# Latent attention's scores: one product over 128 rows a head in place of two over 64 and 32 rows

## The chip, the cores and the metric

The kernel runs on one core of a Trainium2 chip. The metric is the device time of one execution in microseconds. Several executions are timed, and one more is taken with the hardware profiler, which gives the rows shown below. TensorE (PE) multiplies, VectorE (DVE) and ScalarE (ACT) do the elementwise work and empty the accumulators (PSUM banks), SyncE (SP) issues the loads, and GpSimd (POOL) issues the gathers at the end.

## What is computed

Two blocks run one after the other on 256 tokens of 1024 features, in float32. The first block has two layers; each holds a gated recurrence of eight heads (HGRN), a causal latent attention of eight heads (MLA), and a cross-attention to a memory. The second block (a dilated attention, a pooling mixer and a routed feed-forward that gathers 256 rows of 2048 floats for each of 128 partitions) isn't touched by the change. The part that matters:

```python
q = (_rmsnorm(cq, q_norm) @ w_uq).reshape(B, S, 8, 64 + 32)
q_nope, q_rope = q[..., :64], _rope(q[..., 64:], cos, sin)
c = _rmsnorm(ckv, kv_norm)
k_nope = (c @ w_uk).reshape(B, S, 8, 64)
v = (c @ w_uv).reshape(B, S, 8, 64)
k_rope = _rope(kr, cos, sin)              # one key of 32 for all heads
s = (einsum(q_nope, k_nope) + einsum(q_rope, k_rope)) / sqrt(96)
p = softmax(where(causal, s, -1e30)); o = einsum(p, v)
# _rope: [t1*cos - t2*sin, t1*sin + t2*cos] over the two halves of 16
```

## The kernel before, in words

Weights stream through three buffers as half units of 128x1024 floats. Each is loaded on SP's queue (`raw`, L167), rounded by ScalarE into `wh` (L159), and the remainder is taken by VectorE into `wl` (L160); a product is then three passes on TensorE (`mm3`, L213 to L215). After each half unit `tick` emits side work: Python generators that stand in a list and yield an estimated cost, against a credit per tick. `mla_qkv`, `mla_rest`, `mla_attend`, the HGRN levels (L328 to L390) and the gates are such side work. `behind` (`bh` in the code) ties a VectorE instruction in order, without a semaphore, behind the newest split `wl` that was emitted. The framework then orders each engine's instructions by a simulation of its own, and each engine works through its list strictly in order.

In a layer, `layer` loads `ws`, the small weights of the latent attention (L636), forms the latent rows (`misc`), and starts the side work. `mla_rest` transposes the latents (L499), projects q in three banks (L512) that ScalarE empties into `qn` and `qr` (L514, L516), k in two banks into `kn` (L522, L523), v in two (L527, L528), rotates `qr` by a product with a permutation (L532) and three VectorE steps (L536, L537, L539), and rotates the shared key into `kr`, repeated four times down the partitions (L543 to L553). `lnr`, the rows of the layer norm, has the buffer of `ws`, so its load (L641) waits on SP's queue for the last product that reads `ws`.

`mla_attend` calls `attend` eight times, for two blocks of queries and four pairs of heads (h, h+4). Each call writes the scores of two heads into one bank. A head takes one product over 64 rows (`qn`, `kn`, L563) and one over 32 rows (`qr`, `kr`, L565), which accumulate; there are 128 keys for the first block of queries and 256 for the second. A float32 product is two MATMUL instructions in the trace. Then come the mask, the softmax, the transposes (L437) and the product with v (L461).

Of the kernel before, what the change touches and what calls it, by code (L numbers as in the profile page):

```python
# [8 lines left out]
F = mybir.dt.float32  # L9
# [3 lines left out]
AF = mybir.ActivationFunctionType  # L13
OP = mybir.AluOpType
# [4 lines left out]
S = 256  # L19
D = 1024  # L20
# [77 lines left out]
def pack(inp):  # L98

    g = {k: np.asarray(v) for k, v in inp.items()}  # L100
    o = {}
    o["ca"], o["cb"] = _shape_constants()
    o["x"] = g["x"].reshape(2, 128, D).transpose(1, 0, 2)
    o["memT"] = g["mem"][0].T.reshape(8, 128, S).transpose(1, 0, 2)
    o["pos"] = g["positions"].reshape(1, S)
    wu, wm, ws = [], [], []
    for l in range(NL):
        w = g["w_in"][l]
        m = w[:, OCQ:OMG].reshape(2, 4, 128, 416).transpose(0, 2, 1, 3).reshape(2, 128, 1664)
        wm.append(m)  # L110
        u = _fm(g["w_mem_k"][l], 0, 512) + _tm(g["w_mem_v"][l], 0, 512)
        pair = lambda j: _fm(w, OF + 256 * j, 256) + _fm(w, OQ + 256 * j, 256)
        u += pair(0) + _tm(w, OI, 512) + pair(1) + _tm(w, OG, 512) + pair(2) + _tm(w, OI + 512, 512) + pair(3)
        u += _fm(w, OMQ, 512) + _tm(w, OG + 512, 512) + _tm(w, OMEMG, 512) + _tm(w, OMG, 512)
        wo = g["w_out"][l].reshape(4, 4, 128, 2, 512)
        for kg in KORD:
            for cg in range(2):
                u.append(wo[kg, :, :, cg].transpose(1, 0, 2).reshape(128, 2048))
        wu.append(np.stack(u))
        uq = g["w_mla_uq"][l].reshape(2, 128, 8, 96)  # L120
        uq = np.concatenate([uq[..., :64].reshape(2, 128, 512), uq[..., 64:].reshape(2, 128, 256)], axis=-1)
        ws.append(np.concatenate([uq.transpose(1, 0, 2).reshape(128, 1536), g["w_mla_uk"][l], g["w_mla_uv"][l]], axis=1))
    o["wu"], o["wm"], o["ws"] = np.stack(wu), np.stack(wm), np.stack(ws)
    o["rows1"] = np.concatenate([g["hgrn_out_norm"], g["mla_q_norm"], g["mla_kv_norm"], g["ln_g"], g["ln_b"]], axis=1)
    o["lnc"] = np.stack([g["ln_g"], g["ln_b"]], axis=1).reshape(2, 2, 8, 128).transpose(3, 0, 1, 2)
    o["lbl"] = g["hgrn_lb_logits"].reshape(2, 8, 128).transpose(2, 0, 1)
    cols = [g["c_2"].reshape(8, 128).T, g["norm1_g_2"].reshape(8, 128).T, g["norm2_g_2"].reshape(8, 128).T,
            g["pool_scale_2"].reshape(4, 128).T, g["b_ada_2"].reshape(48, 128).T]
    o["cols2"] = np.concatenate(cols, axis=1)
    o["rows2"] = np.concatenate([g["b_ada_2"][0, 2048:3072], g["b_ada_2"][0, 5120:6144], g["final_g_2"]]).reshape(1, 3072)  # L130
    o["wada"] = g["w_ada_2"][0].reshape(8, 128, 6, 1024).transpose(2, 0, 1, 3)
    w2 = g["w_in_2"][0]
    u = _fm(w2, 0, 1024) + _tm(w2, 1024, 1024)
    wo = g["w_out_2"][0].reshape(2, 4, 128, 2, 512)
    for kg in (1, 0):
        for cg in range(2):
            u.append(wo[kg, :, :, cg].transpose(1, 0, 2).reshape(128, 2048))
    u += _fm(g["peer_wq_2"][0], 0, 2048)
    o["wu2"] = np.stack(u)
    o["ws2"] = np.concatenate([g["pool_w_2"][0].transpose(1, 0, 2).reshape(128, 512),  # L140
                               g["peer_subkeys_2"][0].transpose(2, 0, 1).reshape(128, 256)], axis=1)
    o["puv"] = np.concatenate([g["peer_u_2"][0], g["peer_v_2"][0]], axis=1)
    return {k: np.ascontiguousarray(v) for k, v in o.items()}


class Prog:
# [346 lines left out]
    def mla_rest(self, ws, cn, out):  # L493
        nc, bh = self.nc, self.behind
        cT = self.ml.tile([128, 3, S], F, name="cT")
        for k in range(3):
            ps = self.pps.tile([128, S], F, name="bank")
# [1 line left out]
                nc.tensor.transpose(ps[:, tt * 128:(tt + 1) * 128], cn[:, tt, k * 128:(k + 1) * 128], self.ident)  # L499
            nc.scalar.activation(cT[:, k, :], ps, AF.Copy)  # L500
            yield 0.3
        sc = 1.0 / math.sqrt(96)
        qn = self.ml.tile([128, 4, S], F, name="qn")
        qr = self.ml.tile([128, 2, S], F, name="qr")
        kn = self.ml.tile([128, 4, S], F, name="kn")
        v = self.ml.tile([128, 2, 512], F, name="v")
        for j in range(3):
            ps = self.pps.tile([128, 2, S], F, name="bank")
            for m in range(2):
                for k in range(2):  # L510
                    c = k * 768 + (2 * j + m) * 128
                    nc.tensor.matmul(ps[:, m, :], ws[:, c:c + 128], cT[:, k, :], start=k == 0, stop=k == 1)  # L512
            if j < 2:
                nc.scalar.activation(qn[:, 2 * j:2 * j + 2, :], ps, AF.Copy, scale=sc)  # L514
            else:
                nc.scalar.activation(qr, ps, AF.Copy, scale=sc)  # L516
            yield 0.6
        for j in range(2):
            ps = self.pps.tile([128, 2, S], F, name="bank")
            for m in range(2):  # L520
                c = 1536 + (2 * j + m) * 128
                nc.tensor.matmul(ps[:, m, :], ws[:, c:c + 128], cT[:, 2, :], start=True, stop=True)  # L522
            nc.scalar.activation(kn[:, 2 * j:2 * j + 2, :], ps, AF.Copy)  # L523
            yield 0.6
        for tt in range(2):
            ps = self.pps.tile([128, 512], F, name="bank")
            nc.tensor.matmul(ps, cT[:, 2, tt * 128:(tt + 1) * 128], ws[:, 2048:2560], start=True, stop=True)  # L527
            nc.scalar.activation(v[:, tt, :], ps, AF.Copy)  # L528
            yield 0.6

        ps = self.pps.tile([128, 2, S], F, name="bank")
        nc.tensor.matmul(ps, self.perm, qr, start=True, stop=True)  # L532
        tmp = self.h2.tile([128, 2, S], F, name="pt")
        sb = self.sin[:, None, :].to_broadcast([128, 2, S])
        cb = self.cos[:, None, :].to_broadcast([128, 2, S])
        bh(nc.vector.tensor_tensor(tmp, ps, sb, op=OP.mult))  # L536
        bh(nc.vector.tensor_tensor(qr, qr, cb, op=OP.mult))  # L537
        yield 1.2
        bh(nc.vector.tensor_tensor(qr, qr, tmp, op=OP.add))  # L539
        yield 0.6  # L540
        ps = self.pps.tile([32, S], F, name="bank")
        for tt in range(2):
            nc.tensor.transpose(ps[:, tt * 128:(tt + 1) * 128], cn[:, tt, 384:416], self.ident)  # L543
# [2 lines left out]
        ps = self.pps.tile([128, 2, S], F, name="bank")  # L546
        nc.tensor.matmul(ps[:, 0, :], self.rep[:32, :], kr0, start=True, stop=True)
        nc.tensor.matmul(ps[:, 1, :], self.reps[:32, :], kr0, start=True, stop=True)
        kr = self.ml.tile([128, S], F, name="kr")
        tk = self.h2.tile([128, S], F, name="pt")  # L550
        bh(nc.vector.tensor_tensor(kr, ps[:, 0, :], self.cos, op=OP.mult))
        bh(nc.vector.tensor_tensor(tk, ps[:, 1, :], self.sin, op=OP.mult))
        bh(nc.vector.tensor_tensor(kr, kr, tk, op=OP.add))  # L553
        out += [qn, qr, kn, kr, v]
        yield 1.0

    def mla_attend(self, qkv, y):
        nc = self.nc
        qn, qr, kn, kr, v = qkv

        def score(ps, h, tt, nk):
            a, c = h // 2, (h % 2) * 64
            nc.tensor.matmul(ps, qn[c:c + 64, a, tt * 128:(tt + 1) * 128], kn[c:c + 64, a, :nk], start=True, stop=False)  # L563
            a, c = h // 4, (h % 4) * 32
            nc.tensor.matmul(ps, qr[c:c + 32, a, tt * 128:(tt + 1) * 128], kr[c:c + 32, :nk], start=False, stop=True)  # L565

        def bias(s, ps, heads, tt):
            n = len(heads)
# [61 lines left out]
    def layer(self, l, x, xt, mem):  # L630
        nc, I = self.nc, self.I
        W = I["wu"][l]
        rows = self.h4.tile([128, 512], F, name="rowsa", bufs=1)
        nc.sync.dma_start(rows, I["rows1"][l:l + 1, 0:512].to_broadcast([128, 512]))
        ws = self.ml.tile([128, 2560], F, name="ws")
        nc.sync.dma_start(ws, I["ws"][l])  # L636
        pm = self.misc(l, xt)
        qkv = []
# [35 lines left out]
        v = values()  # L674
# [3 lines left out]
        g = self.silu_gate(tok())  # L678
# [4 lines left out]
        v = values()  # L683
# [49 lines left out]
        if l == NL - 1:  # L733
            self.drain()
            self.ahead = self.unit(I["wu2"][0][:, 0:1024])
            ss = [self.sm.tile([128, 3], F, name="nss") for _ in range(2)]
        for tt in range(2):
            residual(tt, 0)
# [62 lines left out]
    def setup(self, cp, c0):  # L801
# [39 lines left out]
        self.pin = nc.scalar.preload_act_table_set("natural_log_exp_and_others")  # L841
        self.tc.add_manual_dep(self.pin.ins, last.ins.name, NOSYNC, reason="the set is loaded behind the sines")
        nc.vector.tensor_scalar(self.sin, self.sin, cols[:, 1:2], None, op0=OP.mult)

        lg = cp.tile([128, 2, 8], F, name="lg")
        nc.sync.dma_start(lg, I["lbl"])
# [378 lines left out]
def body(tc, I, O, stop=None):  # L1225
    nc = tc.nc
    p = Prog(tc, I)
    with tc.tile_pool(name="c0", bufs=1) as c0, tc.tile_pool(name="wp", bufs=3) as wp, \
# [4 lines left out]
        with tc.tile_pool(name="mo", bufs=1) as mo:  # L1233
            xnp = tc.alloc_tile_pool(name="xnp", bufs=1)
            gp = tc.alloc_tile_pool(name="gp", bufs=1)
            p.xn = xnp.tile([128, 2, D], F, name="xn")
            with tc.tile_pool(name="cp", bufs=1) as cp, tc.tile_pool(name="xtp", bufs=4) as xtp, tc.tile_pool(name="h4", bufs=3) as h4, \
                    tc.tile_pool(name="h2", bufs=2) as h2, tc.tile_pool(name="ml", bufs=1) as ml:
                p.xtp, p.h4, p.h2, p.ml = xtp, h4, h2, ml
# [47 lines left out]
```

## Time and profile before

| | us |
|---|---|
| median of 3 runs | 1469.14 (1466.65 to 1471.23) |
| profiled execution | 1465.43 |
| its span, first to last instruction | 1463.7 |
| PE busy in the span | 1292.2 (88%) |
| DVE busy | 1014.7 (69%) |
| ACT busy | 591.9 (40%) |

The time of the profiled execution is 1.7 us more than its span. "PE busy" counts matmuls whose ends are modelled, so a busy PE can still be short of its best rate; PEld is the loading of the stationary operand, which can overlap the product before it.

### The profile page before, as it was taken

Reading aid. Unit: us, or ns where it says so; the run is one execution under the profiler, and the core shown is the slowest. Engines: PE = TensorE matmul, PEld = TensorE weight load, DVE = VectorE, ACT = ScalarE, POOL = GpSimd, SP = SyncE. Lnnn points to the kernel's source line nnn. Section 1 sums busy time; section 2 is a strip of 40 time slices with the busy share of each in tenths; the row PEclk is TensorE's granted clock in tenths of the full one; section 3 lists DMA queues with packets and bytes.
Section 4 is the critical chain, followed back from the end, with each engine's and each line's share of the span. In section 5 each row is a group of like instructions: output and inputs, shape, how many; then the busy total and the mean of one; then the engine's idle time right before and its main releaser. Section 6 shows DMA issues by size and latency. Waiting matters only on the chain.

```text
span 1463.7 us, 17364 instructions
## 1 busy us (share of the span) xinstructions
PE 1292.2 (88%) x5834; PEld 882.2 (60%) x5834; DVE 1014.7 (69%) x2039; ACT 591.9 (40%) x1288; POOL 243.5 (17%) x260
## 2 busy tenths in 40 slices
PE   8999999998999999989997997786888777878776
PEld 7888897777887888878677733232333333333332
DVE  6487689767578787576566777777776977755554
ACT  5556556535566576344544422222222322211112
POOL 0000000000000000000003243333334333333330
PEclk9999999999999999999998999999889898999988
DMA  8564255576562453556538799999999999999993
GB/s 290 167 208 129 87 172 163 178 242 220 165 188 87 130 159 101 173 197 214 179 123 343 290 423 421 421 421 421 421 421 421 377 421 421 422 420 422 422 421 158
DMA packets 74537, 404.79 MB, mean 277 GB/s; under 512 B 8912, under 2 KB 9296, under 8 KB 40784
## 3 DMA queue, kind: packets, MB, share of 16 engines
q0 software_dynamic: 36864, 268.45, 44.3%
q1 hardware_dynamic: 37584, 135.23, 28.2%
q8 instruction: 47, 0.77, 0.2%
q14 instruction: 42, 0.34, 0.1%
HBM read 402.60 MB, written 1.05 MB: 276 GB/s over the span
## 4 chain that ended last, share of the span: by engine, by line
PE 49%; DMA 36%; DVE 7%; issue 3%; ACT 3%; POOL 0%; DVEq 0%; POOLq 0%; ACTq 0%
DMA uv<-in_puv_dram,eid 31%; PE bank L214 9%; PE bank L213 9%; PE bank L215 9%; PE acc L1218 7%; DMA raw<-in_wu_dram 4%; PE bank L371 3%; ACT wh L159 2%; PE bank L461 2%; DVE uv L1208 2%; DVE wl L160 1%; PE bank L221 1%; PE bank L565 1%; PE bank L563 1%; PE bank L437 1%
## 5 line engine op out<-in xcount | busy, mean ns | idle before, releaser
L1218 PE MATMUL acc<-uv,d 128*128 128x512 f32 x1024 | 501.7, 649 | 126.1 <-ACT d L1216 125.7
L1218 PEld LDWEIGHTS acc<-uv,d 128*128 128x128 f32 x1024 | 207.6, 208 | 415.3 <-issue 245.5
L1174 POOL DMA_INDIRECT uv<-in_puv_dram,eid x256 | 243.3, 950 | 1183.1 <-DVE eid L1113 774.5
L1208 DVE CUSTOM_DVE_ANT_0 uv<-hid,uv 128x1024 f32<-128x1024 f32 x256 | 313.2, 1223 | 180.7 <-DMA uv<-in_puv_dram,eid 172.2
L160 DVE TENSOR_TENSOR wl<-raw,wh 128x1024 fp32r<-128x1024 f32 (+1 forms) x184 | 223.2, 1214 | 123.9 <-ACT wh L159 115.5
L159 ACT ACTIVATE wh<-raw 128x1024 fp32r<-128x1024 f32 (+1 forms) x184 | 192.8, 1050 | 196.1 <-DMA raw<-in_wu_dram 79.6
L1211 ACT ACTIVATE dot<-dot 128x4 f32<-128x4 f32 (+1 forms) x66 | 13.5, 205 | 408.9 <-DVE dot L1208 408.8
L213 PE MATMUL bank<-wh,xh 128*128 128x512 f32 (+1 forms) x400 | 161.6, 405 | 1.2 <-ACT xh L258 0.8
L214 PE MATMUL bank<-wl,xh 128*128 128x512 f32 (+1 forms) x400 | 160.0, 400 | 2.0 <-DVE wl L160 2.0
L215 PE MATMUL bank<-wh,xl 128*128 128x512 f32 (+1 forms) x400 | 159.1, 398 | 0.0
L213 PE MATMUL bank<-xh,wh 128*128 128x256 f32 x384 | 113.5, 296 | 3.8 <-ACT wh L159 3.8
L215 PE MATMUL bank<-xh,wl 128*128 128x256 f32 x384 | 110.6, 288 | 4.8 <-DVE wl L160 4.8
L214 PE MATMUL bank<-xl,wh 128*128 128x256 f32 x384 | 110.6, 288 | 0.0
L1216 ACT ACTIVATE d<-ident,dot 128x128 f32<-128x128 f32 x256 | 82.8, 390 | 39.9 <-DVE dot L1212 34.0
L214 PEld LDWEIGHTS bank<-wl,xh 128*128 128x128 f32 x400 | 75.6, 189 | 18.5 <-DVE wl L160 3.4
L213 PEld LDWEIGHTS bank<-wh,xh 128*128 128x128 f32 x400 | 75.6, 189 | 16.6 <-ACT xh L258 1.0
L215 PEld LDWEIGHTS bank<-wh,xl 128*128 128x128 f32 x400 | 75.6, 189 | 15.7 <-issue 0.7
L213 PEld LDWEIGHTS bank<-xh,wh 128*128 128x128 f32 x384 | 73.9, 192 | 6.8 <-ACT wh L159 4.8
L215 PEld LDWEIGHTS bank<-xh,wl 128*128 128x128 f32 x384 | 73.7, 192 | 6.4 <-DVE wl L160 6.0
L214 PEld LDWEIGHTS bank<-xl,wh 128*128 128x128 f32 x384 | 73.9, 192 | 1.8 <-issue 1.2
L213 PE MATMUL bank<-nh,wh 128*128 128x256 f32 x192 | 58.5, 305 | 1.1 <-issue 0.7
L214 PE MATMUL bank<-nl,wh 128*128 128x256 f32 x192 | 56.5, 295 | 1.4 <-DVE nl L259 1.4
(286 smaller groups left out, 1715.1 us busy)
## 6 DMA issues: line engine op xcount, KB each, us to landing
raw<-in_wu_dram SPq DMA_DIRECT2D x176, 512.0 KB, 4.2
raw<-in_wada_dram SPq DMA_DIRECT2D x48, 512.0 KB, 3.5
uv<-in_puv_dram,eid POOLq DMA_INDIRECT x256, 18.0
raw<-in_wm_dram SPq DMA_DIRECT2D x8, 416.0 KB, 4.0
ws<-in_ws_dram SPq DMA_DIRECT2D x2, 1280.0 KB, 9.2
raw<-in_memT_dram SPq DMA_DIRECT2D x4, 512.0 KB, 4.6
lnr<-in_rows_dram SPq DMA_DIRECT2D x2, 1024.0 KB, 7.9
cb<-in_cb_dram SPq DMA_DIRECT2D x1, 1408.0 KB, 6.0
```

The source lines that it names most:

```text
L159: nc.scalar.activation(wh[:, :n], raw[:, :n], AF.Copy)
L160: self.last_split = nc.vector.tensor_tensor(wl[:, :n], raw[:, :n], wh[:, :n].bitcast(F), op=OP.subtract)
L213: mm(ps, a[0], b[0], start=start, stop=False)
L214: mm(ps, a[0], b[1], start=False, stop=False)
L215: self.last_mm = mm(ps, a[1], b[0], start=False, stop=stop)
L221: m = self.nc.tensor.matmul(ps, self.zero, self.zero[:, None, :].to_broadcast([128, 4, 128]), start=True, stop=True)
L371: nc.tensor.matmul(ps[:, h, k, :], st[:, c:c + 128], mv[:, c:c + 128], start=True, stop=True)
L461: nc.tensor.matmul(po[:, i, :], pt[:, i * kb + k, :], v[:, k, h * dv:(h + 1) * dv], start=k == 0, stop=k == kb - 1)
L1174: nc.gpsimd.indirect_dma_start(out=t, out_offset=None, in_=I["puv"], in_offset=bass.IndirectOffsetOnAxis(ap=eid[:, u, k:k + 1], axis=0))
L1208: self.last_split = nc.vector.tensor_tensor_reduce(out=uv[:, 0:D], in0=hid, in1=uv[:, 0:D], scale=1.0, scalar=0.0, op0=OP.mult, op1=OP.add ...
L1216: nc.scalar.activation(d, self.ident, AF.Copy, scale=dot[:, u, k:k + 1])
L1218: nc.tensor.matmul(acc[:, cg * 512:(cg + 1) * 512], d, uv[:, D + cg * 512:D + (cg + 1) * 512], start=u % 8 == 0 and k == 0, stop=u % 8 == ...
```

## The change

The weights of q are packed per head as 128 columns: 64 plain ones, the 32 rotary ones, and the rotary ones again with their halves exchanged. So q comes out of four banks as eight tiles of 128 rows, and one VectorE multiplication by a table `turn` (scale; scale times cosine; scale times signed sine) empties each bank. The key tile `kt` has the head's 64 plain rows below and the rotated shared key twice above, copied in for all heads by two ScalarE instructions. The score of a head is then one product over 128 rows. The product with the permutation and the three VectorE steps of the rotation of q go. k is projected head by head into 64 columns; k and v come after the rotation of the key. `ws` grows from 2560 to 3072 floats a partition. `kt` takes the buffer that `xn`, a tile used from the end of the second layer on, held alone; `xn` is allocated when it is needed. The change's short description also names routing steps tied behind dot products; no line of the diff touches the routing.

```diff
@@ pack
-        uq = np.concatenate([uq[..., :64].reshape(2, 128, 512), uq[..., 64:].reshape(2, 128, 256)], axis=-1)
+        uq = np.concatenate([uq, uq[..., 80:], uq[..., 64:80]], axis=-1).reshape(2, 128, 1024)
@@ mla_rest
-        qn = self.ml.tile([128, 4, S], F, name="qn")
-        qr = self.ml.tile([128, 2, S], F, name="qr")
-        kn = self.ml.tile([128, 4, S], F, name="kn")
+        q = self.ml.tile([128, 8, S], F, name="q")
+        kt = self.xnp.tile([128, 8, S], F, name="kt", tag="xn")
-        for j in range(3):
+        for j in range(4):
...
-            if j < 2:
-                nc.scalar.activation(qn[:, 2 * j:2 * j + 2, :], ps, AF.Copy, scale=sc)
-            else:
-                nc.scalar.activation(qr, ps, AF.Copy, scale=sc)
+            bh(nc.vector.tensor_tensor(q[:, 2 * j:2 * j + 2, :], ps, self.turn[:, None, :].to_broadcast([128, 2, S]), op=OP.mult))
...
-        nc.tensor.matmul(ps, self.perm, qr, start=True, stop=True)
-        bh(nc.vector.tensor_tensor(tmp, ps, sb, op=OP.mult))
-        bh(nc.vector.tensor_tensor(qr, qr, cb, op=OP.mult))
-        bh(nc.vector.tensor_tensor(qr, qr, tmp, op=OP.add))
...
+        for j in range(2):
+            nc.scalar.activation(kt[64:, 4 * j:4 * j + 4, :], kr[64:, None, :].to_broadcast([64, 4, S]), AF.Copy)
+        for j in range(4):
+            ps = self.pps.tile([64, 2, S], F, name="bank")
+            for m in range(2):
+                c = 2048 + (2 * j + m) * 64
+                nc.tensor.matmul(ps[:, m, :], ws[:, c:c + 64], cT[:, 2, :], start=True, stop=True)
+            nc.scalar.activation(kt[:64, 2 * j:2 * j + 2, :], ps, AF.Copy)
+            yield 0.3
+        # v as before, now last
@@ mla_attend, score
-            nc.tensor.matmul(ps, qn[c:c + 64, a, tt * 128:(tt + 1) * 128], kn[c:c + 64, a, :nk], start=True, stop=False)
-            nc.tensor.matmul(ps, qr[c:c + 32, a, tt * 128:(tt + 1) * 128], kr[c:c + 32, :nk], start=False, stop=True)
+            nc.tensor.matmul(ps, q[:, h, tt * 128:(tt + 1) * 128], kt[:, h, :nk], start=True, stop=True)
@@ layer
-        ws = self.ml.tile([128, 2560], F, name="ws")
+        ws = self.ml.tile([128, 3072], F, name="ws")
@@ setup
+        self.turn = cp.tile([128, S], F, name="turn")
+        nc.vector.memset(self.turn[:64, :], sc)
+        nc.vector.tensor_scalar(self.turn[64:96, :], self.cos[64:96, :], sc, None, op0=OP.mult)
+        nc.vector.tensor_scalar(self.turn[96:, :], self.sin[96:, :], sc, None, op0=OP.mult)
```

## Rows read from the trace of the kernel before

**Rows 1.** Page, the span in 40 slices: busy tenths of PE.

```profile
PE   8999999998999999989997997786888777878776
```

**Rows 2.** Stages: us, busy (instructions) of PE, PEld, DVE, ACT, POOL; clock; DMA.

```profile
420.00:490.00 70.00, 69.97 (x443) 57.18 (x442) 51.48 (x95) 42.23 (x106) 0.00 (x0) 0.98 0.35 108
...
112.00:138.50 26.50, 26.36 (x186) 23.01 (x184) 20.46 (x39) 18.19 (x45) 0.00 (x0) 1.00 0.42 139
138.50:175.00 36.50, 36.50 (x209) 28.20 (x208) 25.74 (x50) 20.48 (x52) 0.00 (x0) 0.91 0.23 73
```

**Rows 3.** Chain that ended last, 110 to 200 us: start, us, what.

```profile
111.49 0.89 PE bank L371 x8
112.38 0.41 PE bank L563 x2
112.79 0.41 PE bank L565 x2
...
114.04 0.31 PE bank L213
114.35 0.11 PE bank L214
...
138.72 0.63 PE bank L563 x2
...
169.63 0.62 PE bank L565 x2
```

**Rows 4.** Instructions by line and shape, whole span.

```profile
L565 PE MATMUL bank<-kr,qr 32*128 32x256 f32 x32 | 11.3, 434 | 0.0
```

**Rows 5.** Chain, 50 to 110 us: the projections and small products.

```profile
52.71 4.75 PE bank L512 x22
...
63.69 0.86 PE bank L532 x2
...
90.59 0.61 PE bank L374 x8
91.20 0.31 PE bank L213
```

**Rows 6.** Three short stretches of the layers; columns as in rows 2.

```profile
160.50:163.90 3.40, 3.40 (x14) 3.11 (x14) 2.63 (x5) 1.72 (x7) 0.00 (x0) 0.50 0.25 65
170.70:174.10 3.40, 3.40 (x15) 3.17 (x15) 1.38 (x3) 3.12 (x7) 0.00 (x0) 0.51 0.41 134
464.30:467.70 3.40, 3.40 (x13) 2.68 (x12) 2.29 (x5) 0.57 (x2) 0.00 (x0) 0.50 0.15 60
```

**Rows 7.** DVE and ACT in order of time; idle before in brackets.

```profile
60.16 1.23 DVE L160 TENSOR_TENSOR wl<-raw,wh 128x1024 fp32r<-128x1024 f32 x1 [8.24 <-ACT wh L159]
64.58 0.69 DVE L536 TENSOR_TENSOR pt<-bank,sin 128x512 f32<-128x512 f32 x1 [1.79 <-PE bank L532]
...
58.36 0.60 ACT L523 ACTIVATE kn<-bank 128x512 f32<-128x512 f32 x1 [0.27 <-PE bank L522]
59.07 1.06 ACT L159 ACTIVATE wh<-raw 128x1024 fp32r<-128x1024 f32 x1
```

**Rows 8.** SP's queue, the two loads of `lnr`, and what the first waited for.

```profile
63.72 0.33 SPq L641 DMA_DIRECT2D lnr<-in_rows_dram  x1
377.21 0.33 SPq L641 DMA_DIRECT2D lnr<-in_rows_dram  x1
SPq L641 <- PE bank L527: 0.6, 1, 0.6
```

**Rows 9.** The load of `ws`: size and landing; its second issue, its first use.

```profile
ws<-in_ws_dram SPq DMA_DIRECT2D x2, 1280.0 KB, 9.2
352.07 0.33 SPq L636 DMA_DIRECT2D ws<-in_ws_dram  x1
364.41 5.78 PE L512 MATMUL bank<-cT,ws 128*128 128x256 f32 x24
```

**Rows 10.** The instructions that write the rotated key last: ns, first and last start.

```profile
L553 DVE TENSOR_TENSOR kr<-kr,pt x2: 398/400/402, 77.0 to 390.5; 128x256 f32<-128x256 f32 x2
```

More of the change, by code (lines that the diff above doesn't have):

```diff
@@ L120, in pack @@
         uq = g["w_mla_uq"][l].reshape(2, 128, 8, 96)
-        uq = np.concatenate([uq[..., :64].reshape(2, 128, 512), uq[..., 64:].reshape(2, 128, 256)], axis=-1)
-        ws.append(np.concatenate([uq.transpose(1, 0, 2).reshape(128, 1536), g["w_mla_uk"][l], g["w_mla_uv"][l]], axis=1))
+        uq = np.concatenate([uq, uq[..., 80:], uq[..., 64:80]], axis=-1).reshape(2, 128, 1024)
+        ws.append(np.concatenate([uq.transpose(1, 0, 2).reshape(128, 2048), g["w_mla_uk"][l], g["w_mla_uv"][l]], axis=1))
     o["wu"], o["wm"], o["ws"] = np.stack(wu), np.stack(wm), np.stack(ws)
@@ L501, in mla_rest @@
             yield 0.3
-        sc = 1.0 / math.sqrt(96)
-        qn = self.ml.tile([128, 4, S], F, name="qn")
-        qr = self.ml.tile([128, 2, S], F, name="qr")
-        kn = self.ml.tile([128, 4, S], F, name="kn")
+        q = self.ml.tile([128, 8, S], F, name="q")
+        kt = self.xnp.tile([128, 8, S], F, name="kt", tag="xn")
         v = self.ml.tile([128, 2, 512], F, name="v")
-        for j in range(3):
+        for j in range(4):
             ps = self.pps.tile([128, 2, S], F, name="bank")
@@ L510, in mla_rest @@
                 for k in range(2):
-                    c = k * 768 + (2 * j + m) * 128
+                    c = k * 1024 + (2 * j + m) * 128
                     nc.tensor.matmul(ps[:, m, :], ws[:, c:c + 128], cT[:, k, :], start=k == 0, stop=k == 1)
-            if j < 2:
-                nc.scalar.activation(qn[:, 2 * j:2 * j + 2, :], ps, AF.Copy, scale=sc)
-            else:
-                nc.scalar.activation(qr, ps, AF.Copy, scale=sc)
+            bh(nc.vector.tensor_tensor(q[:, 2 * j:2 * j + 2, :], ps, self.turn[:, None, :].to_broadcast([128, 2, S]), op=OP.mult))
             yield 0.6
[L518 to L531, printed above, removed]
-        nc.tensor.matmul(ps, self.perm, qr, start=True, stop=True)
-        tmp = self.h2.tile([128, 2, S], F, name="pt")
-        sb = self.sin[:, None, :].to_broadcast([128, 2, S])
-        cb = self.cos[:, None, :].to_broadcast([128, 2, S])
-        bh(nc.vector.tensor_tensor(tmp, ps, sb, op=OP.mult))
-        bh(nc.vector.tensor_tensor(qr, qr, cb, op=OP.mult))
-        yield 1.2
-        bh(nc.vector.tensor_tensor(qr, qr, tmp, op=OP.add))
-        yield 0.6
         ps = self.pps.tile([32, S], F, name="bank")
@@ L548, in mla_rest @@
         nc.tensor.matmul(ps[:, 1, :], self.reps[:32, :], kr0, start=True, stop=True)
-        kr = self.ml.tile([128, S], F, name="kr")
         tk = self.h2.tile([128, S], F, name="pt")
+        bh(nc.vector.tensor_tensor(tk, ps[:, 1, :], self.sin, op=OP.mult))
+        kr = self.h2.tile([128, S], F, name="pt")
         bh(nc.vector.tensor_tensor(kr, ps[:, 0, :], self.cos, op=OP.mult))
-        bh(nc.vector.tensor_tensor(tk, ps[:, 1, :], self.sin, op=OP.mult))
         bh(nc.vector.tensor_tensor(kr, kr, tk, op=OP.add))
-        out += [qn, qr, kn, kr, v]
         yield 1.0
+        for j in range(2):
[7 more added lines that the diff above has]
+            yield 0.3
+        for tt in range(2):
+            ps = self.pps.tile([128, 512], F, name="bank")
+            nc.tensor.matmul(ps, cT[:, 2, tt * 128:(tt + 1) * 128], ws[:, 2560:3072], start=True, stop=True)
+            nc.scalar.activation(v[:, tt, :], ps, AF.Copy)
+            yield 0.6
+        out += [q, kt, v]
     def mla_attend(self, qkv, y):
         nc = self.nc
-        qn, qr, kn, kr, v = qkv
+        q, kt, v = qkv
         def score(ps, h, tt, nk):
-            a, c = h // 2, (h % 2) * 64
-            nc.tensor.matmul(ps, qn[c:c + 64, a, tt * 128:(tt + 1) * 128], kn[c:c + 64, a, :nk], start=True, stop=False)
-            a, c = h // 4, (h % 4) * 32
-            nc.tensor.matmul(ps, qr[c:c + 32, a, tt * 128:(tt + 1) * 128], kr[c:c + 32, :nk], start=False, stop=True)
+            nc.tensor.matmul(ps, q[:, h, tt * 128:(tt + 1) * 128], kt[:, h, :nk], start=True, stop=True)
         def bias(s, ps, heads, tt):
@@ L735, in layer @@
             self.ahead = self.unit(I["wu2"][0][:, 0:1024])
+            self.xn = self.xnp.tile([128, 2, D], F, name="xn")
             ss = [self.sm.tile([128, 3], F, name="nss") for _ in range(2)]
@@ L843, in setup @@
         nc.vector.tensor_scalar(self.sin, self.sin, cols[:, 1:2], None, op0=OP.mult)
+        sc = 1.0 / math.sqrt(96)
+        self.turn = cp.tile([128, S], F, name="turn")
+        nc.vector.memset(self.turn[:64, :], sc)
+        nc.vector.tensor_scalar(self.turn[64:96, :], self.cos[64:96, :], sc, None, op0=OP.mult)
+        nc.vector.tensor_scalar(self.turn[96:, :], self.sin[96:, :], sc, None, op0=OP.mult)
         lg = cp.tile([128, 2, 8], F, name="lg")
@@ L1235, in body @@
             gp = tc.alloc_tile_pool(name="gp", bufs=1)
-            p.xn = xnp.tile([128, 2, D], F, name="xn")
+            p.xnp = xnp
             with tc.tile_pool(name="cp", bufs=1) as cp, tc.tile_pool(name="xtp", bufs=4) as xtp, tc.tile_pool(name="h4", bufs=3) as h4, \
```

## The prediction, made before the changed kernel ran

> **What bounds the kernel now.** I read the page's slices first: in the first half of the span, where the two layers run, TensorE is busy nine tenths of nearly every slice [rows 1]. Cutting the layers into stages shows where the latent attention sits, in 112 to 175 us and 420 to 490 us. In the first two stretches TensorE is busy for 26.36 of 26.5 and 36.50 of 36.5 us, VectorE for 20.46 and 25.74, ScalarE for 18.19 and 20.48; the second layer looks alike, and the DMA share is at most 0.42 [rows 2]. So TensorE sets the pace there, and VectorE is next. A busy PE need not stream, so the third view is the chain that ended last. It runs through TensorE in this stretch, and it shows what a score costs: one product over 64 or over 32 rows (two MATMULs, x2) takes 0.41 us with 128 keys and 0.62 to 0.63 with 256, each starting only when the one before has run out [rows 3]. By shape there are 32 MATMULs with 256 keys on L565 [rows 4]; L563 and the 128 keys have as many each, so there are 16 products of each kind. In the same chain, products over all 128 rows go faster: eight MATMULs of 128 columns in 0.89, 0.223 a product [rows 3], and twenty-two of 256 columns in 4.75, 0.432 a product [rows 5]. The small products therefore pay about 0.19 us each above their columns. And the first streaming matmul after a block of scores takes 0.31 where the next takes 0.11: 0.20 more on leaving [rows 3].
>
> These rows disagree with a rule that speaks against the change. The Trainium skill, "TensorE: Matmul & The Clock Gate", Part 3, says that products over few rows, placed on distinct row groups, run at the same time. By it a pair would cost one product, the merging would save nothing, and the extra projections below would make the kernel slower. Here the starts are 0.41 apart; the trace doesn't agree. The Trainium skill, "TensorEngine Tiling (Array Packing)", Key Properties, says that changing the tiling mode drains the engine, and 64 and 32 rows are two modes; the 0.19 agrees with that.
>
> **The change part by part**, for both layers.
>
> Scores. A block of two heads is now four products: 4 x 0.415 = 1.66 for 128 keys, 2.50 for 256, and 0.20 on leaving. After, it is two products at the full-array price: 0.45 and 0.86, in the mode of the stream on either side. Saved: 1.66 + 0.20 - 0.45 = 1.41 and 2.50 + 0.20 - 0.86 = 1.84 a block. There are eight blocks of each: 8 x 3.25 = **-26.0**. Were the exit not saved it would be -22.8.
>
> Permutation. One product of 512 columns goes in each layer, 0.86 [rows 5]: **-1.7**.
>
> Projection of q. 16 products instead of 12, 0.432 each: 4 x 0.432 x 2 = **+3.5**.
>
> Projection of k. Eight products of 64 output columns instead of four of 128; the streamed columns are the same 256, so four more products: 3.5. It also goes to a half-wide array. The HGRN product that does this (L374, eight MATMULs of 64 columns) takes 0.61, where eight at the rate of L371, halved, are 0.45; after it the stream's matmul takes 0.31 instead of 0.11 [rows 5, 3]. I take one visit a layer, 0.16 + 0.20, in sum 0.7: **+4.2**. From below, no switch: 3.5. From above, four visits a layer, 2.9: 6.4.
>
> TensorE in sum: -26.0 - 1.7 + 3.5 + 4.2 = **-20.0**.
>
> The clock. Three stretches of 3.4 us in the attention have half the clock (0.50, 0.51, 0.50; 1.2 instead of 2.4 GHz), with TensorE recorded as busy throughout [rows 6]. The second begins 0.5 us after a 256-key block ended at 170.25 [rows 3], in which the array paid 0.19 four times over. Each costs 1.7 us. The cause is only likely, and other such blocks have no dip. I count two of three as going: **-3.4**, between 0 and -5.1.
>
> VectorE. Emptying q takes four multiplications of 128x512 out of PSUM. The rotation's three go, the first of the very same form, 0.69 [rows 7]: one more, +0.7 us a layer on an engine that is not the bound. But TensorE's gain brings VectorE near. The 128-key blocks lie in 112 to 138.5, 26.5 us with 20.46 of VectorE; less 4 x 1.41 leaves 20.9, 98% of it [rows 2]; the 256-key stretch, 36.5 - 7.4 = 29.1 with 25.74, leaves room. VectorE can hardly follow without a gap, and the softmax chains have less time to hide, so I take 1 us a layer given back: **+2.0**. Below 0; above, the whole saving of the 128-key blocks, 8 x 1.41 = 11.3.
>
> ScalarE. Five copies of 0.60 a layer become four, plus two copies of the key of 1024 columns by 64 partitions; nearest row: 1.06 for 128x1024 [rows 7]. That is 4.5 instead of 3.0. Queued behind them is the rounding of the next weights, for which VectorE's remainder and then TensorE wait. ScalarE has 24 of 63 us free in the attention [rows 2]: nothing, with 1.5 a layer if the cover were gone (3.0).
>
> New waits. The third and fourth bank of q wait until VectorE has emptied the first two, behind a split. In the first layer VectorE then stands idle for 8.24 us [rows 7]. TensorE's list holds stream products to put between, so I cost it at nothing; see the second rival. The load of `lnr` waits for the last reader of `ws`, now the v products behind the key's rotation. The raw loads queue behind it on SP; it waited 0.6 us [rows 8], and I cost its move at nothing; see the third rival.
>
> Front. `ws` is 20% larger. It landed in 9.2 us, in the second layer at 361.3; at 11.0 it is 363.1, and q's first product stands at 364.41 [rows 9]. In the first layer it is early. Two short VectorE steps for `turn` come in the setup, each no dearer than the 0.40 of L553 [rows 10], and the stream's loads share the DMA with `ws`: **+0.6**, between 0 and 2.6 (0.8, and 1.8 for the load).
>
> Sum: -20.0 - 3.4 + 2.0 + 0.6 = **-20.8**. On the profiled execution's own 1465.4 (span 1463.7 and 1.7 around it) that is 1444.6. The median of the runs is 3.7 higher, and runs are compared by it: 1469.1 - 20.8 = 1448.3. The rest of the span (second block, gathers) moves forward unchanged.
>
> **The rivals.** *VectorE becomes the bound.* For it: 98% in the stretch above. Against it: 88% in the 256-key stretch, and little added. It gives back up to the 11.3: -20.0 - 3.4 + 11.3 + 0.6 = -11.5, about 1457.6. Chance 0.10.
>
> *Banks of q stall behind splits.* If the last banks are tied behind a split that itself waits for weights TensorE has still to use up, TensorE's list can't be filled, and the idle 8.24 becomes TensorE's, twice: -20.8 + 16.5 = -4.3, about 1464.8. Against it: VectorE stood idle for those 8.24 us with nothing before it in its list, so a bank tied behind an earlier split is emptied at once. Chance 0.04.
>
> *`lnr` holds the loads* (the other side). The key's rotation ends at 77.4 and 390.9 [rows 10]; k and v behind it (8 x 0.432, and 4 MATMULs of 512 columns, 1.7) end about 5.2 later. If the load kept its place at 63.7 and 377.2 [rows 8], SP would stand for about 19 us a layer. With one half unit in hand (24 matmuls of 0.11 to 0.12, 2.8 us [rows 3]) TensorE starves for 16: +32 - 20.8 = +11, about 1480. It decides from 12.6 us of starving a layer (25.2 in all, less 20.8, is 4.4). With all three buffers filled, 8.4, it is 10.6 a layer, and the time is unchanged. Against it: in the first layer SP waited 0.6 us for it [rows 8], so its place on SP follows the release. Chance 0.05.
>
> *Small products overlap after all*: the 64-row and the 32-row product of a head run through the array together, so the scores save nothing, and 3.5 + 4.2 - 1.7 = +6.0 stays, 1475. The 0.41 between starts speaks against it. Chance 0.01. It is what the Trainium skill's "TensorE: Matmul & The Clock Gate", Part 3, would have.
>
> **How the numbers follow.** The forecast has 0.80, between 1469.1 - 26 (exit saved, all dips gone, no give-back: -20.7 - 5.1) = 1443 and 1469.1 - 12 (k at its upper bound, exit not saved, no dip gone: -14.6 + 2.6) = 1457. The range takes in the VectorE rival, the stretch between it and the next, and a few us below for chains that tighten: 1440 to 1462. About 0.3% (4.4 us) is what a measurement here tells from no change. Faster: 0.80 + 0.10 and part of the stall, 0.91. Same: the rest of it and `lnr` with cover, 0.05. Slower: 0.04.
>
> **What would show it.** Score products at 0.22 and 0.43, with the stream's matmul after them at 0.11; 32 products on one line in place of 64 on two. L512's successor 32 MATMULs a layer; k 16 a layer, with one slow matmul after them. In 112 to 175, now some 13 us shorter, VectorE's share near 0.9. The three half-clock stretches fewer. The forecast is wrong if score products keep 0.41, if TensorE's idle time before `wl` or q's banks grows in that stretch by more than 5 us a layer, or if SP waits more than some us at `lnr`.

## The result, and the profile after

The changed kernel's median is 1454.57 us over 7 runs (1449.0 to 1459.06), against 1469.14 over 7 runs of the kernel before: a ratio of 0.9894, 95% interval 0.9866 to 0.9922, that is 11.5 to 19.7 us less. The forecast was 1448.3, 20.8 us less, with a range of 1440 to 1462. Its profiled execution took 1449.26 with a span of 1447.5.

The page of the changed kernel, its first and second parts: busy us, share and instructions; then 40 slices.

```profile
PE 1263.4 (87%) x5798; PEld 868.2 (60%) x5798; DVE 1015.0 (70%) x2044; ACT 593.6 (41%) x1290; POOL 244.0 (17%) x260
...
PE   8999999988999999989988987777787777878786
```

TensorE's busy time fell by 28.8 us from 1292.2 and VectorE's did not move. The chain of the changed kernel in the two attention stretches of the first layer answers to [rows 3] (start, us, what):

```profile
120.09 0.50 PE bank L549 x4
120.59 0.12 PE bank L215
...
135.47 0.92 PE bank L549 x4
136.39 0.23 PE bank L214
```

L549 is the one score product. A block of two heads takes 0.50 us with 128 keys and 0.92 with 256, where it took 1.66 and 2.50, and the streaming matmul behind it comes at its usual 0.12 or 0.23: the 0.20 on leaving is gone. The chain of the projections answers to [rows 5]:

```profile
52.45 6.48 PE bank L510 x30
62.46 0.69 PE bank L520 x2
...
63.59 1.01 PE bank L534 x4
64.60 0.32 PE bank L213
65.15 1.87 PE bank L534 x8
67.02 0.32 PE bank L213
68.52 1.01 PE bank L534 x4
69.52 1.05 PE bank L539 x2
```

q runs at the old rate, 0.432 a product. k (L534) enters the half-wide mode three times a layer, not once, and each visit pays on entering (1.01 for four MATMULs, where four cost 0.86 before) and on leaving (0.32 where the stream has 0.12; v's pair 1.05 where such a pair is 0.86).

The stages of the attention, first the whole of it in both layers, then the two stretches of the first layer that answer to [rows 2] (us, busy of PE, PEld, DVE, ACT, POOL; clock; DMA):

```profile
110.00:165.00 55.00, 53.76 (x383) 47.58 (x382) 47.95 (x91) 39.22 (x100) 0.00 (x0) 1.00 0.40 126
412.00:475.00 63.00, 62.26 (x452) 56.03 (x451) 53.76 (x104) 44.27 (x122) 0.00 (x0) 1.00 0.39 127
...
112.00:136.00 24.00, 23.64 (x179) 21.93 (x178) 20.03 (x38) 18.77 (x44) 0.00 (x0) 1.00 0.51 160
136.00:165.00 29.00, 28.12 (x196) 24.02 (x195) 26.70 (x53) 19.92 (x55) 0.00 (x0) 1.00 0.28 92
```

Three things are to be seen. The clock is 1.00 throughout, where three stretches at half clock stood before [rows 6]. VectorE is busy for 26.70 of 29 us, 92%, in the stretch of the 256-key blocks. And TensorE now has gaps: 1.24 of 55 us are idle. The line that sums the chain by engine and line in 132 to 165 us says the same:

```profile
by line: DMA raw<-in_wu_dram 12.2%; PE bank L371 11.6%; PE bank L461 10.1%; PE bank L549 8.4%; PE bank L215 7.8%; PE bank L214 7.1%; DVE t L341 6.9%; PE bank L437 5.9%; PE bank L213 5.7%; DVE qk L343 3.7%; DVE wl L160 3.4%; DVE at L390 3.3%
```

A load of weights, a scan, a product and a split on VectorE have places in a chain that ran through TensorE before, as the same line for 138 to 175 us of the kernel before shows:

```profile
by line: PE bank L563 13.5%; PE bank L565 13.5%; PE bank L214 13.2%; PE bank L215 12.6%; PE bank L213 12.2%; PE bank L371 9.6%; PE bank L461 8.2%; PE bank L437 4.3%; PE bank L405 4.2%; PE bank L404 3.5%; PE bank L374 2.7%; PE bank L402 2.4%
```

Three pieces of the changed kernel's chain show the order: a scan and then a split (`wl`) on VectorE, and a load of weights behind them.

```profile
154.18 1.13 DVE t L341
155.37 1.13 DVE wl L160
156.55 4.03 DMA raw<-in_wu_dram
```

SP's queue, the loads of `lnr` and what the two waited for in sum, answers to [rows 8]:

```profile
77.22 0.33 SPq L625 DMA_DIRECT2D lnr<-in_rows_dram  x1
381.48 0.33 SPq L625 DMA_DIRECT2D lnr<-in_rows_dram  x1
...
SPq L625 <- PE bank L539: 3.6, 2, 1.8
```

The load was issued 13.5 and 4.3 us later, with the product that it waits for; SP stood 1.8 us at most.

The runs spread over some 10 us, so single stages are read here from a landmark as well: the start of the second layer's layer norm (L754 before, L739 after), where the work that the change touches is over. The rows give ns of one, first and last start; the first three are of the kernel before in its two profiles and of the changed kernel, the fourth of the changed kernel's second profile (the first experiment below).

```profile
L754 DVE SCALAR_TENSOR_TENSOR x<-x,bag,lnr x4: 744/749/753, 619.0 to 625.1; 128x512 f32<-128x512 f32 x4
```

```profile
L754 DVE SCALAR_TENSOR_TENSOR x<-x,bag,lnr x4: 744/747/752, 623.0 to 629.1; 128x512 f32<-128x512 f32 x4
```

```profile
L739 DVE SCALAR_TENSOR_TENSOR x<-x,bag,lnr x4: 744/749/753, 601.2 to 607.3; 128x512 f32<-128x512 f32 x4
```

```profile
L739 DVE SCALAR_TENSOR_TENSOR x<-x,bag,lnr x4: 744/750/754, 602.7 to 608.7; 128x512 f32<-128x512 f32 x4
```

So the two layers became 16.3 to 21.8 us shorter. From there to the end the four profiles take 844.7, 847.0, 846.3 and 844.7 us: the rest of the span moved forward as a whole, and its own spread of some 2 us is part of the spread of the runs.

Much of the landmark's own spread is the clock. Stretches at half clock (0.50 or 0.51) ahead of it, inside the attention and outside, add up to 17.1, 27.3, 0 and 3.4 us in these four profiles. TensorE was recorded as busy for nearly all of that time, so about half of it was lost. With that half taken off, the landmark stands at 610.5 and 609.4 us before and at 601.2 and 601.0 after. This estimate, called the landmark at full clock below, makes the change worth 8.2 to 9.5 us; the rest of what was gained up to there is half-clock time that is gone.

The second thing that differs is how long TensorE sat idle ahead of the landmark. The rows have the columns of [rows 2]; the first two are of the two profiles before, the next two of the two after, and the last two belong to an experiment below (VectorE relieved: before, then after):

```profile
0.00:619.00 619.00, 604.70 (x3680) 512.87 (x3681) 447.23 (x723) 354.32 (x729) 0.20 (x4) 0.99 0.52 169
0.00:623.00 623.00, 607.93 (x3680) 517.17 (x3681) 447.22 (x722) 354.68 (x729) 0.20 (x4) 0.98 0.52 168
0.00:601.20 601.20, 580.33 (x3644) 499.63 (x3645) 447.49 (x727) 355.60 (x731) 0.20 (x4) 1.00 0.54 175
0.00:602.70 602.70, 581.59 (x3644) 499.51 (x3645) 447.57 (x728) 355.43 (x731) 0.20 (x4) 1.00 0.54 174
...
0.00:623.00 623.00, 606.67 (x3680) 515.22 (x3681) 438.58 (x698) 352.92 (x729) 0.20 (x4) 0.98 0.52 167
0.00:597.90 597.90, 581.06 (x3644) 501.33 (x3645) 439.31 (x704) 354.84 (x731) 0.20 (x4) 0.99 0.54 176
```

The idle time is 14.3 and 15.1 us before, 20.9 and 21.1 after.

### The profile page after: what moved, and what is told of

It reads as the page before. It is cut to its first block, busy times and chain, and to the rows that moved or that the text cites. A ratio compares the mean times of both kernels' runs of the same rounds, so it can differ in the third digit from the quotient of the medians.

```text
span 1447.5 us, 17295 instructions
## 1 busy us (share of the span) xinstructions
PE 1263.4 (87%) x5798; PEld 868.2 (60%) x5798; DVE 1015.0 (70%) x2044; ACT 593.6 (41%) x1290; POOL 244.0 (17%) x260
## 3 DMA queue, kind: packets, MB, share of 16 engines
HBM read 403.12 MB, written 1.05 MB: 279 GB/s over the span
## 4 chain that ended last, share of the span: by engine, by line
PE 45%; DMA 37%; DVE 9%; ACT 4%; issue 4%; POOL 0%; DVEq 0%; ACTq 0%; POOLq 0%; SPq 0%
DMA uv<-in_puv_dram,eid 31%; PE bank L214 8%; PE bank L213 8%; PE bank L215 8%; PE acc L1209 8%; DMA raw<-in_wu_dram 6%; PE bank L371 2%; ACT wh L159 2%; DVE uv L1199 2%; DVE wl L160 2%; PE bank L461 2%; PE bank L221 1%; PE bank L510 1%; PE bank L437 1%; PE bank L549 1%
## 5 line engine op out<-in xcount | busy, mean ns | idle before, releaser
L1209 PE MATMUL acc<-uv,d 128*128 128x512 f32 x1024 | 495.2, 641 | 129.2 <-ACT d L1207 129.2
L1202 ACT ACTIVATE dot<-dot 128x4 f32<-128x4 f32 (+1 forms) x66 | 13.5, 205 | 406.5 <-DVE dot L1199 406.4
L213 PE MATMUL bank<-xh,wh 128*128 128x256 f32 x384 | 110.6, 288 | 4.3 <-ACT wh L159 4.3
```

The costliest lines, as they stand in the source:

```text
L213: mm(ps, a[0], b[0], start=start, stop=False)
L1209: nc.tensor.matmul(acc[:, cg * 512:(cg + 1) * 512], d, uv[:, D + cg * 512:D + (cg + 1) * 512], start=u % 8 == 0 and k == 0, stop=u % 8 == ...
```

## The experiments

**The changed kernel again**, on the chip of the next three.

> The changed kernel itself, on the chip of the next three runs. Both theories: 0.987 to 0.992 of the kernel before, some 13 to 19 us less, with no half-clock stretch in the attention of either layer.

0.9885 of the kernel before (0.9859 to 0.9910; medians 1451.16 and 1467.84), and the clock is 1.00 in both attention stretches. Both medians together put the change at 14.6 to 16.7 us.

**Four small products a block, in one mode.** The plain part of the score is taken twice, the rotary part left out.

```diff
-            nc.tensor.matmul(ps, q[:, h, tt * 128:(tt + 1) * 128], kt[:, h, :nk], start=True, stop=True)
+            for c in (0, 1):
+                nc.tensor.matmul(ps, q[:64, h, tt * 128:(tt + 1) * 128], kt[:64, h, :nk], start=c == 0, stop=c == 1)
```

> Changed kernel with each score taken as two products over the 64 plain rows of the head, one accumulated on the other (the rotary part of the score is left out). So a block again has four products of 64 rows, as before, but all in one mode. Theory A (changing between 64 and 32 rows is what costs): the four follow each other at 0.22 us with 128 keys and 0.43 with 256, with 0.2 on entering and 0.2 on leaving; a block takes 1.3 or 2.1 with its exit, 8 x (0.84 + 1.27) = 17 us more than the changed kernel. Theory B (any product under 128 rows pays 0.19): 0.41 and 0.62 a product as before, 1.86 or 2.70 a block, 8 x (1.41 + 1.84) = 26 us more.

Its chain (start, us, what):

```profile
117.05 1.09 PE bank L550 x8
118.14 0.32 PE bank L213
...
138.89 1.92 PE bank L550 x8
```

Four products of 64 rows take 1.09 and 1.92, where four that alternate between 64 and 32 rows took 1.66 and 2.50. Beyond the columns (0.89 and 1.73) there is one price of 0.19 to 0.20 on entering and one of 0.20 on leaving. So the few rows are not what cost: the change of mode is. A block before paid it on entering, three times inside and on leaving. Which rows the two products of a head use made no difference: heads 0, 3, 4 and 7 have them partly on the same rows, the others on distinct ones, and every block at full clock took 1.66 or 2.50. The time agrees: 0.9984 of before (0.9962 to 1.0006) against 0.9885, a difference of 14.5 us, 10 to 20 with both intervals taken together. Theory A's 17 is within, theory B's 26 is not. The profile alone shows less: its landmark (614.9, with 10.2 us of half clock ahead) is at 609.8 at full clock, about 8.7 later than the changed kernel's, and TensorE's idle time ahead of it is 17.1 us, some 4 less. So part of the added work went where the changed kernel lost time. This is what the Trainium skill has in "TensorEngine Tiling (Array Packing)", Key Properties: a change of tiling mode drains the engine. The trace agrees, with about 0.2 us on entering and on leaving.

**The score product issued twice.**

```diff
             nc.tensor.matmul(ps, q[:, h, tt * 128:(tt + 1) * 128], kt[:, h, :nk], start=True, stop=True)
+            nc.tensor.matmul(ps, q[:, h, tt * 128:(tt + 1) * 128], kt[:, h, :nk], start=True, stop=True)
```

> Changed kernel with each score product over 128 rows issued twice, the second writing the same numbers over the first. TensorE gets 8 x (0.45 + 0.86) = 10.5 us of work more, all in the attention, in one mode. Theory TensorE still sets the pace there: 10 to 11 us more. Rival, VectorE and the softmax chains set it since the change (part of the saving was given back): under 6 us more, and TensorE's idle time in the attention falls.

0.9938 (0.9909 to 0.9967): 7.8 us more than the changed kernel, 2 to 13 with both intervals. That lies between the two theories and settles neither. TensorE was idle for 0.14 of 63 us in the attention of the first layer, less than in the changed kernel, as the rival has it. The landmark (612.8, with 10.2 us of half clock ahead) is at 607.7 at full clock, 6.6 later than in the changed kernel, again between the two.

**k in pairs of heads.** A product over 128 columns for two heads; ScalarE brings the second head's half down to rows 0 to 63.

```diff
-        for j in range(4):
-            ps = self.pps.tile([64, 2, S], F, name="bank")
+        for j in range(2):
+            ps = self.pps.tile([128, 2, S], F, name="bank")
             for m in range(2):
-                c = 2048 + (2 * j + m) * 64
-                nc.tensor.matmul(ps[:, m, :], ws[:, c:c + 64], cT[:, 2, :], start=True, stop=True)
-            nc.scalar.activation(kt[:64, 2 * j:2 * j + 2, :], ps, AF.Copy)
-            yield 0.3
+                c = 2048 + (2 * j + m) * 128
+                nc.tensor.matmul(ps[:, m, :], ws[:, c:c + 128], cT[:, 2, :], start=True, stop=True)
+            for o in range(2):
+                nc.scalar.activation(kt[:64, 4 * j + o:4 * j + 4:2, :], ps[64 * o:64 * o + 64], AF.Copy)
+            yield 0.6
```

> Changed kernel with k projected for two heads at a time into 128 columns, each head's half copied to rows 0 to 63 by ScalarE; eight products a layer become four, and the half-wide mode is not entered. k takes 3.89 us and three exits of 0.2 a layer in the changed kernel, 1.72 should remain: 2 x 2.8 = 5.5 us less for TensorE. Theory the projections stand on TensorE's path: 5 to 6 us less than the changed kernel. Rival, the stretch behind them takes it back: under 2 us.

> The paired kernel again, beside the two above: 0.984 to 0.989 of the kernel before, as in its first run.

Its chain:

```profile
63.40 1.06 PE bank L534 x4
64.46 0.12 PE bank L213
64.81 0.86 PE bank L534 x4
65.67 0.12 PE bank L213
```

k takes 1.92 us a layer and no exit. With the changed kernel's three visits (1.01 + 1.87 + 1.01 = 3.89) and their three exits (0.20 + 0.20 + 0.19 = 0.59) that is 2 x (3.89 + 0.59 - 1.92) = 5.1 us less for TensorE. The time is 0.9864 of before (0.9838 to 0.9890), and 0.9854 (0.9820 to 0.9888) in the second run. Against the changed kernel's 0.9885 that is 3 to 4.5 us better, inside the intervals: by the time neither the 5 to 6 nor the under 2 is decided. The landmark of its two profiles:

```profile
L740 DVE SCALAR_TENSOR_TENSOR x<-x,bag,lnr x4: 744/748/752, 605.0 to 611.0; 128x512 f32<-128x512 f32 x4
L740 DVE SCALAR_TENSOR_TENSOR x<-x,bag,lnr x4: 744/750/752, 598.4 to 604.5; 128x512 f32<-128x512 f32 x4
```

They differ by 6.6 us, with 20.5 and 6.8 us of half clock ahead, none of it in the attention. At full clock they stand at 594.8 and 595.0, about 6.2 before the changed kernel's 601.2 and 601.0: that is for the 5 to 6. By its ratio it is the fastest version here, and both of its intervals lie below 1.

**VectorE relieved.** The steps that cap exponentials are left out, in the changed kernel and in the kernel before.

```diff
-            self.behind(nc.vector.tensor_scalar(g, g, float(2.0 ** 62), None, op0=OP.min))
...
-        bh(nc.vector.tensor_scalar(e, e, float(2.0 ** 62), None, op0=OP.min))
```

> Changed kernel without the twelve VectorE minimum steps a layer that cap exponentials (0.42 to 0.43 us each; the caps are left out), so VectorE has 5.1 us a layer less and TensorE the same. Theory the change left VectorE and the softmax chains setting the pace for part of the layers: the layer norm of the second layer starts 3 to 6 us earlier than in the changed kernel (601.2 and 602.7 us in its two profiles). Rival, TensorE alone: under 1.5 us.

> The same twelve steps a layer left out of the kernel before. Both theories: TensorE sets the pace, so the layer norm of the second layer starts within 1.5 us of 619.0, and the time is within 0.3% of before, apart from half-clock stretches.

The landmark, first of the changed kernel, then of the kernel before, each without the caps:

```profile
L737 DVE SCALAR_TENSOR_TENSOR x<-x,bag,lnr x4: 744/747/752, 597.9 to 603.9; 128x512 f32<-128x512 f32 x4
```

```profile
L752 DVE SCALAR_TENSOR_TENSOR x<-x,bag,lnr x4: 744/750/752, 623.0 to 629.1; 128x512 f32<-128x512 f32 x4
```

The changed kernel gets there 3.3 and 4.8 us before its two profiles. That alone would say little, since two profiles of one kernel differ by up to 6.6 us. With 6.8 us of half clock ahead it stands at 594.5 at full clock, 6.5 to 6.7 before the changed kernel's. TensorE's idle time ahead of the landmark falls from 20.9 and 21.1 to 16.8 us, and its gaps in the attention close. The load, the scan and the split are gone from the chain of 132 to 165 us, whose twelve largest lines are all TensorE's. The kernel before gets there at 623.0, later than the 1.5 us around 619.0 that were expected; 20.5 us of half clock lie ahead, and at full clock it stands at 612.8, no earlier than its own 610.5 and 609.4. Its idle time stays, 16.3 against 14.3 and 15.1. That is as the theory of a shared bound has it: these 10 us of VectorE's work are free to take away before, and worth about 6 after. The whole times neither show it nor speak against it: the ratios are 0.9889 (0.9847 to 0.9930) on this chip against 0.9885 for the changed kernel on another, the medians 20.1 us below the kernel before against 16.7, and the kernel before without caps has 1.0004 (0.9982 to 1.0026). Each version has one profile, so the size is less sure than the direction.

**q's banks emptied by ScalarE**, with the scale alone (the rotation of q is left out).

```diff
-            bh(nc.vector.tensor_tensor(q[:, 2 * j:2 * j + 2, :], ps, self.turn[:, None, :].to_broadcast([128, 2, S]), op=OP.mult))
+            nc.scalar.activation(q[:, 2 * j:2 * j + 2, :], ps, AF.Copy, scale=1.0 / math.sqrt(96))
```

> Changed kernel with the banks of q emptied by ScalarE with the scale alone (the rotation of q is left out). VectorE loses 2.8 us a layer, ScalarE gets 2.4. Theory the banks on VectorE were hidden: within 1.5 us of the changed kernel at the second layer's layer norm. Rival, the banks stalled TensorE behind the splits: 3 us or more less, and the q products follow each other faster than 6.48 us for thirty.

The thirty q MATMULs take 6.48 us again, to the hundredth, so VectorE emptied the banks without holding TensorE. The time is 0.9898 (0.9861 to 0.9936), no better than the changed kernel. Its landmark, 607.6, is later than forecast; four half-clock stretches, 13.7 us, lie ahead of it in that profile, outside the attention. At full clock it stands at 600.8, within the 1.5 us of the changed kernel.

**The kernel before, profiled once more.**

> The kernel before, profiled once more. Theory the half-clock stretches in the attention come from the small score products: stretches at 0.50 again near 160, 170 and 464 us. Rival, they fall where they will from run to run: other places, or none in the attention.

The attention of both layers in this profile, then in that of the kernel before without caps, in the changed kernel's second profile, and in the first layer of the kernel with four small products in one mode (columns as above):

```profile
110.00:178.00 68.00, 67.97 (x413) 55.88 (x411) 49.59 (x93) 39.61 (x97) 0.00 (x0) 0.92 0.31 101
420.00:495.00 75.00, 74.98 (x467) 61.91 (x467) 54.09 (x99) 45.36 (x117) 0.00 (x0) 0.95 0.36 118
```

```profile
110.00:178.00 68.00, 67.89 (x414) 54.77 (x414) 47.88 (x89) 39.08 (x97) 0.00 (x0) 0.95 0.33 109
420.00:495.00 75.00, 74.89 (x471) 61.42 (x469) 53.45 (x97) 45.04 (x118) 0.00 (x0) 0.98 0.36 114
```

```profile
110.00:165.00 55.00, 54.27 (x384) 47.88 (x382) 49.14 (x93) 38.79 (x97) 0.00 (x0) 1.00 0.40 126
412.00:475.00 63.00, 62.30 (x445) 55.67 (x444) 53.08 (x106) 45.19 (x121) 0.00 (x0) 1.00 0.42 134
```

```profile
110.00:172.00 62.00, 61.92 (x423) 53.98 (x423) 50.48 (x94) 42.11 (x114) 0.00 (x0) 1.00 0.37 121
```

A mean clock of 0.92 over 68 us is 68 x 0.08 x 2 = 11 us at half rate. By such sums the three profiles with alternating scores have about 7, 11 and 7 us at half clock in the first layer's attention and 3, 7 and 3 in the second's, at places that differ from run to run. All ten profiles whose scores stay in one mode have 1.00 there, in both layers. So neither expectation held to the letter: the places are not fixed, but in the attention the stretches come with the alternating scores. Elsewhere in the layers both kinds of kernel have them. Why the clock falls just there is not shown.

**The side work's pace**, on the kernel with k in pairs.

```diff
-PACE_A = 1.4
+PACE_A = 1.8   # and 1.1 in the second
```

> The kernel with k in pairs, and the side work paced at 1.8 per tick instead of 1.4 in the layers, so that gates and attention are emitted earlier. Theory the saving is given back where side work is still open late in the layer: the first layer's layer norm starts 2 us or more before the paired kernel's 334.9 and the time falls by 2 to 5 us. Rival, VectorE is filled earlier and starves the stream: slower by 2 us or more.

> The kernel with k in pairs, and the side work paced at 1.1 per tick. Theory of open side work: 2 us or more slower than the paired kernel. Rival, VectorE too dense in the attention: 2 us or more faster.

0.9867 (0.9838 to 0.9895) and 0.9859 (0.9831 to 0.9886), against 0.9854 for the paired kernel beside them: no difference clear of intervals of some 4 us. The first layer's layer norm starts at 334.4 and 333.3, against 334.9 and 329.9 in the two paired profiles. The theory of open side work isn't borne out either way: the faster pace brings no gain, the slower one no loss. In the profiles the landmark at full clock is 598.0 with 1.8, about 3 later than the paired kernel's, as the rival has it, and 595.1 with 1.1, no different. One profile each doesn't decide 3 us.

## Why the prediction was right, point by point

**The bound and the price of a score: right.** TensorE set the pace of the layers before: VectorE's work could be left out for nothing. A small score product paid about 0.19 us above its columns, and the one-mode run shows that the change of mode is the cause, as the prediction had it.

**Scores: right.** Forecast -26.0. A block now takes 0.50 and 0.92, not 0.45 and 0.86, so it saves 1.66 + 0.20 - 0.50 = 1.36 and 2.50 + 0.20 - 0.92 = 1.78; 8 x 3.14 = -25.1.

**Permutation and q: right**, -1.7 and +3.5, at the rate of before.

**k: mis-sized, within its bounds.** Forecast +4.2 with one visit to the half-wide mode. There are three a layer, and with their exits they cost 3.89 + 0.20 + 0.20 + 0.19 = 4.48, where k took 1.72; +5.5 in both layers. The framework put stream matmuls between the four banks. TensorE in sum: -25.1 - 1.7 + 3.5 + 5.5 = -17.8, forecast -20.0.

**Clock: right in kind, mis-sized.** Two of three stretches were counted, -3.4. All of them went, -5.1 against the profile shown, and -8.5 against the second profile of before, which had five. The prediction gave no cause that the runs confirm; it called its own only likely.

**Give-back: mis-sized, and put in the wrong stretch.** Forecast +2.0, in the 128-key blocks. Up to the landmark TensorE's terms make -17.8, and the half-clock time that is gone -8.5 in the first pair of profiles and -13.7 + 1.7 = -12.0 in the second: -26.3 and -29.8, where the landmark moved by 601.2 - 619.0 = -17.8 and 602.7 - 623.0 = -20.3. So 8.5 and 9.5 us came back. Of that, 6.6 and 6.0 stand as TensorE's idle time; the rest does not show as idle. VectorE's share is highest, 92%, in the 256-key stretch, which had been taken to leave room; in the 128-key stretch, counted at 98%, it is 20.03 of 24 us, 83%. That VectorE and the chains through it take most of it is shown, for one profile, by the 6.5 to 6.7 us that its relief gave after the change and not before. Of the idle time only 2.0 us lie in the attention's two stages as shown above; where in the layers the rest arises stays open.

**The hidden parts: right.** q's banks on VectorE held up nothing. The load of `lnr` was issued later, with the product that it waits for, and SP stood 1.8 us at most. The larger `ws` landed in 7.9 and 10.0 us; its second load was issued at 345.04, and q's products began at 357.77. In the first layer they began at 51.7, before the change at 51.9, so the +0.6 for the front does not show. The copies of the key on ScalarE took 1.04 us each, counted at 1.06.

**The sum.** The two medians say -14.6 and -16.7; the forecast of -20.8 stood 4 to 6 us low, and its range of 1440 to 1462 held the time. It stood so near partly by luck: two terms missed in opposite directions. The give-back was 8.5 to 9.5 in place of 2.0, while the half-clock time that went was worth more than the 3.4 counted, 5.1 to 8.5 in the attention alone. None of the rivals came in full. The first, VectorE as the bound, came in good part, though in another stretch than the one it was argued from: relieving VectorE gave about 6.6 of its 11.3, and the median of 1454.57 lies between its 1457.6 and the forecast. The 64-row and 32-row products of a head don't overlap, on the same rows or on distinct ones. The prediction set this against a rule on products over distinct row groups. But the two products are of two modes and write one bank, and half of the heads have them on shared rows, so the trace speaks against that rule for this pairing alone. Pairs in one mode on distinct rows were not tried, and what they would do stays open.

## What to carry to other kernels

Price a small matmul by the distance between starts in the chain, not by its columns: here products of 64 and 32 rows in turn cost five changes of mode a block of two heads, 0.2 us each, and one product over all rows costs little more than its columns (0.50 us a block for 0.45, 0.92 for 0.86). When a busy engine is relieved, add up the next engine's busy time in each stretch that gets shorter, not in the stage as a whole; here VectorE at 92% in one stretch went with 8.5 to 9.5 us given back over two layers. Before comparing two profiles, take out the half-clock time of each: here it hid differences of 6 us between kernels. And look at what the new code brings in of the same kind: the 64-column k products paid three mode visits a layer for what two-head products do without any.

## What the runs showed of the hardware that was not expected

The granted clock can differ between stages in which TensorE is recorded as busy alike: recorded as busy for 67.97 of 68 us, it was granted 0.92 in the attention with alternating 64- and 32-row products, and 1.00 when busy for 61.92 of 62 us with 64-row products in one mode. Emptying a PSUM bank of 64 partitions on ScalarE took about as long as one of 128: 0.59 against 0.60 us for 512 columns.
